# One small store, two issuers: splitting the last output transfer between SyncE and ScalarE

## The chip, the cores and the metric

The kernel runs on one core of one Trainium2 chip. The metric is the device time of one execution in microseconds; the median of 3 runs of the kernel before is 161.53 us (161.51 to 161.56). A profile of one execution gives the times of single instructions: start and duration on TensorE (PE), VectorE (DVE), ScalarE (ACT), GpSimd (POOL) and SyncE (SP). A "q" behind an engine's name (SPq, ACTq) marks what its sequencer does itself: issuing transfers, waiting, loading a register, branching.

## The reference

The kernel computes a log-sum-exp over the last axis of x, 32 × 512 rows of 1024 floats:

```
max_x = np.max(x, axis=-1, keepdims=True)
return (max_x.squeeze(-1) + np.log(np.sum(np.exp(x - max_x), axis=-1))).astype(np.float32)
```

The input is 67 MB, the output 16384 floats (64 KB).

## The kernel before, in words

The 16384 rows are laid out over 128 partitions, 128 rows to a partition: 112 of them (`W`) form the first part of the output, the last 16 (`B`) the second part. The kernel leaves the maximum out at first: it takes exp of x as it is, sums, takes Ln, and raises a flag if any sum is so small or so large that this was not safe. Only if the flag is raised does it recompute everything with the maximum (the block under `nc.If`, lines 304 to 347).

x comes in by 19 loads (`LOADS`), all issued by SyncE at line 141 into a ring of 48 rows per partition. SyncE waits until the part of the ring that a load overwrites has been used. ScalarE takes the exponential of what has landed, in place (line 229). The sums of a row are then made by one of several ways, written out for each load by letters: VectorE sums whole rows (`R`, line 240), GpSimd adds the halves of rows and VectorE sums the rest (`G`, lines 235 and 159), or VectorE adds the halves and sums in one instruction (`T`, line 167). The very last row is split between VectorE (`a`, line 255) and ScalarE, which sums while it exponentiates (`b`, line 224). There is no planner; the order on each engine is the order of the program text.

The end of the program, in which the change lies, runs as follows. When 112 rows per partition are summed, ScalarE takes their Ln (line 202) and SyncE stores them (line 263). For the last 16, ScalarE takes Ln of 15 (line 267) and then of the last one (line 269), whose two part sums are added by the bias; line 272 copies one part sum to where the flag's arithmetic reads it. SyncE waits for line 269 and issues the last store (line 274): 16 floats from each of 128 partitions, 8 KB, counted on a semaphore `stored` that reaches 16 when it has landed.

Beside that the flag is worked out: VectorE at lines 278 and 282, three matmuls at lines 288, 290 and 292 (the last waits for line 272's copy), and a comparison at line 296. ScalarE and VectorE load the flag into a register (line 299) and branch over the recomputation (line 349 is where both go on). Each raises `done`; SyncE waits for both, waits for the early store, clears the kernel's semaphores (line 352), and at last waits for `stored` to reach 16 and subtracts 16 again (line 354). That wait is SyncE's last instruction in the program.

In the whole of this path SyncE alone issues transfers. ScalarE issues some too, but only inside the recomputation.

Of the kernel before, what the change touches and what calls it, by code (L numbers as in the profile page):

```python
# [53 lines left out]
def kernel(  # L54
# [5 lines left out]
    nc = tc.nc  # L60
# [4 lines left out]
    P = nc.NUM_PARTITIONS  # L65
# [9 lines left out]
    NC = n // P  # L75
    H = d // 2
    W = NC - B
# [5 lines left out]
    out_rest = out_flat[P * W : n].rearrange("(p c) -> p c", p=P)  # L83

    def source(e0, size):
        assert e0 >= W * d or e0 + size <= W * d
        return x_rest[:, e0 - W * d : e0 - W * d + size] if e0 >= W * d else x_rows[:, e0 : e0 + size]
# [9 lines left out]
    def sbuf(name, cols, dtype=fp32, rows=P):  # L97
        return nc.alloc_sbuf_tensor(name, [rows, cols], dtype).ap()
# [6 lines left out]
    res = sbuf("res", NC)  # L105
# [10 lines left out]
    act = Counted(nc, nc.scalar, "act")  # L116
# [9 lines left out]
    stored = nc.alloc_semaphore("stored")  # L126
# [53 lines left out]
    for i, (size, parts) in enumerate(loads):  # L180
# [8 lines left out]
        for k, part in enumerate(parts):  # L189
# [8 lines left out]
            if part[0][0] == "L":  # L198
# [4 lines left out]
                    out=res[:, 0:W], in_=sumexp[:, 0:W], func=AF.Ln  # L203
                ))
                continue
            if part[0][0] == "A":
                assert here == p
                for _ in range(part[0][1]):
                    v = ring[:, p : p + d]
                    summed_by_act = act.did(nc.scalar.activation(  # L210
                        out=v, in_=v, func=AF.Exp, accum_out=sumexp[:, c : c + 1]
# [11 lines left out]
            if part[-1][0] == "b":  # L223
                nc.scalar.activation(  # L224
                    out=v, in_=v, func=AF.Exp, accum_out=rest
# [5 lines left out]
            for how, s in part:  # L231
                rows = ring[:, p : p + s * d].rearrange("p (c d) -> p c d", d=d)
                if how == "G":
                    pool.wait(act, at)
                    folded.append((c, p, s, pool.did(nc.gpsimd.tensor_tensor(  # L235
                        out=rows[:, :, 0:H], in0=rows[:, :, 0:H], in1=rows[:, :, H:d], op=ALU.add,
                    ))))
                elif how == "R":
                    dve.wait(act, at)
                    users.append((p, p + s * d, dve, dve.did(nc.vector.reduce_sum(  # L240
                        out=sumexp[:, c : c + s], in_=rows, axis=AX.X
# [27 lines left out]
    ln_last = act.did(nc.scalar.activation(  # L269
        out=res[:, LAST:NC], in_=rest, func=AF.Ln, bias=sumexp[:, LAST:NC]  # L270
    ))
    last = act.did(nc.scalar.copy(out=sumexp[:, REST : REST + 1], in_=rest))  # L272
    sp.wait(act, ln_last)
    nc.sync.dma_start(out=out_rest, in_=res[:, W:NC]).then_inc(stored, 16)

    dve.wait(act, summed_by_act)
    nc.vector.wait_ge(parts_summed, 2)
# [1 line left out]
        out=clamped[:, 0 : LEAST + 1 - checked], in0=sumexp[:, checked : LEAST + 1], scalar=LOW,  # L279
# [3 lines left out]
        out=total, in_=sumexp[:, checked : TOTAL + 1], axis=AX.X  # L283
# [20 lines left out]
    with nc.If(all_fine < 1):  # L304

        nc.scalar.wait_ge(sp.sem, 16)
        nc.scalar.wait_ge(stored, 16)
        rows = 0
        steps = 0
        for c0 in range(0, NC, RING):  # L310
            s = min(RING, NC - c0)
            v = ring[:, 0 : s * d].rearrange("p (c d) -> p c d", d=d)
            neg = clamped[:, c0 : c0 + s]
            if c0:
                nc.scalar.wait_ge(ready, steps)
            edge = max(c0, min(W, c0 + s))
            for c1, c2 in ((c0, edge), (edge, c0 + s)):
                if c1 == c2:
                    continue
                nc.scalar.dma_start(  # L320
                    out=ring[:, (c1 - c0) * d : (c2 - c0) * d],
                    in_=source(c1 * d, (c2 - c1) * d),
                ).then_inc(again, 16)
                rows += 16
            nc.vector.wait_ge(again, rows)
            nc.vector.tensor_reduce(
                out=neg, in_=v, op=ALU.max, axis=AX.X, negate=True
            ).then_inc(ready, 1)
            nc.vector.wait_ge(ready, steps + 1)
            nc.vector.tensor_add(  # L330
                out=v, in0=v, in1=neg[:, :, None].to_broadcast([P, s, d])
            ).then_inc(ready, 1)
            nc.scalar.wait_ge(ready, steps + 2)
            nc.scalar.activation(out=v, in_=v, func=AF.Exp).then_inc(ready, 1)
            nc.vector.wait_ge(ready, steps + 3)
            nc.vector.reduce_sum(
                out=sumexp[:, c0 : c0 + s], in_=v, axis=AX.X
            ).then_inc(ready, 1)
            steps += 4
        nc.scalar.wait_ge(ready, steps)  # L340
        nc.scalar.activation(out=res, in_=sumexp[:, 0:NC], func=AF.Ln).then_inc(ready, 1)
        nc.vector.wait_ge(ready, steps + 1)
        nc.vector.tensor_sub(out=res, in0=res, in1=clamped).then_inc(ready, 1)
        nc.scalar.wait_ge(ready, steps + 2)
        nc.scalar.dma_start(out=out_rest, in_=res[:, W:NC]).then_inc(again, 16)
        nc.scalar.dma_start(out=out_rows, in_=res[:, 0:W]).then_inc(again, 16)
        nc.scalar.wait_ge(again, rows + 32)
# [5 lines left out]
    kind = dict(sync_type="semaphore", id=stored.num, ant_name="stored")  # L353
    nc.sync.add_instruction(mybir.InstEventSemaphore(
        name=nc.get_next_instruction_name(), engine=mybir.EngineType.SP,
        sync_info=mybir.SyncInfo(
            on_wait=[mybir.SyncWait(wait_mode="sem-ge-imm", wait_value=16, **kind)],
            on_update=[mybir.SyncUpdate(update_mode="sem-sub-imm", update_value=16, **kind)],
        ),
    ))  # L360

# [46 lines left out]
```

## Time and profile before

| what | us |
|---|---|
| median of 3 runs | 161.53 |
| the profiled execution | 161.49 |
| its span, first to last instruction of the program | 160.2 |
| VectorE busy | 116.2 |
| ScalarE busy | 114.6 |
| GpSimd busy | 33.3 |
| last store, start of its issue | 158.70 |
| last store, from issue to landing | 1.4 |

The span is what the profile's rows cover; 161.49 less 160.2 leaves 1.3 us that lie around it and that no row shows. The transfers of x fill nearly all of the span: 67.18 MB on one queue, whose packets took 97.9% of the 16 DMA engines' span. In the view of the chain, time is followed back from the instruction that ended last on a computing engine; what SyncE and the sequencers do after that is read from other views: the instructions of one line, the waits of SyncE, and the timeline.

### The profile page before, as it was taken

Reading aid. Unit: us, or ns where it says so; the run is one execution under the profiler, and the core shown is the slowest. Engines: PE = TensorE matmul, PEld = TensorE weight load, DVE = VectorE, ACT = ScalarE, POOL = GpSimd, SP = SyncE. Lnnn points to the kernel's source line nnn. Section 1 sums busy time; section 2 is a strip of 40 time slices with the busy share of each in tenths; the row PEclk is TensorE's granted clock in tenths of the full one; section 3 lists DMA queues with packets and bytes.
Section 4 is the critical chain, followed back from the end, with each engine's and each line's share of the span. In section 5 each row is a group of like instructions: output and inputs, shape, how many; then the busy total and the mean of one; then the engine's idle time right before and its main releaser. Section 6 shows DMA issues by size and latency. Waiting matters only on the chain.

```text
span 160.2 us, 183 instructions
## 1 busy us (share of the span) xinstructions
PE 0.3 (0%) x6; PEld 0.2 (0%) x6; DVE 116.2 (73%) x56; ACT 114.6 (72%) x32; POOL 33.3 (21%) x14
## 2 busy tenths in 40 slices
PE   0000000000000000000000000000000000000000
PEld 0000000000000000000000000000000000000000
DVE  0000000029997599999999699929999999999996
ACT  3000069970999419992799349964998999999996
POOL 0000000000000000000000000990580589996000
DMA  8997999799699699996999999997989999999993
GB/s 272 496 512 336 432 515 466 306 515 498 272 513 513 272 479 478 478 463 268 453 468 468 468 430 430 430 430 332 499 364 472 415 446 395 451 395 431 414 408 105
DMA packets 3025, 67.18 MB, mean 419 GB/s; under 512 B 592, under 2 KB 720, under 8 KB 1488
## 3 DMA queue, kind: packets, MB, share of 16 engines
q1 hardware_dynamic: 3024, 67.18, 97.9%
q14 instruction: 1, 0.01, 0.0%
HBM read 67.11 MB, written 0.07 MB: 419 GB/s over the span
## 4 chain that ended last, share of the span: by engine, by line
DMA 53%; ACT 21%; DVE 18%; POOL 5%; issue 0%; PE 0%; SPq 0%
DMA ring<-in_x_dram 53%; ACT ring L229 21%; DVE sumexp L240 15%; POOL ring L235 5%; DVE sumexp L159 2%; ACT ring L224 0%; SPq L141 0%; DVE clamped L278 0%; PE count L288 0%; ACT res L202 0%; DVE fine L296 0%; PE count L290 0%; PE count L292 0%
## 5 line engine op out<-in xcount | busy, mean ns | idle before, releaser
L229 ACT ACTIVATE ring<-ring 128x16000 f32<-128x16000 f32 (+24 forms) x25 | 112.2, 4546 | 42.7 <-DMA ring<-in_x_dram 42.6
L240 DVE TENSOR_REDUCE sumexp<-ring 128x9 f32<-128x9216 f32 (+7 forms) x10 | 89.8, 9000 | 39.1 <-ACT ring L229 39.1
L235 POOL TENSOR_TENSOR ring<-ring 128x2048 f32<-128x2048 f32 (+5 forms) x8 | 33.0, 4128 | 112.3 <-ACT ring L229 112.2
L159 DVE TENSOR_REDUCE sumexp<-ring 128x4 f32<-128x2048 f32 (+5 forms) x8 | 16.5, 2079 | 3.4 <-POOL ring L235 3.4
L167 DVE SCALAR_TENSOR_TENSOR ring<-ring 128x512 f32<-128x512 f32 (+1 forms) x16 | 9.8, 672 | 0.0
L128 ACT ACT_TABLE_LOAD x1 | 1.3, 1283 | 1.4 <-PEq L63 1.4
L167 DVE DVE_READ_ACCUMULATOR ring<-ring 128x1 f32 x16 | 1.3, 82 | 0.0
L224 ACT ACTIVATE ring<-ring 128x480 f32<-128x480 f32 x1 | 0.6, 602 | 0.0
L288 PE MATMUL count<-far,bad 128*1 128x1 f32 x2 | 0.2, 165 | 158.7 <-DVE clamped L278 158.7
L176 DVE TENSOR_REDUCE sumexp<-sumexp 128x1 f32<-128x106 f32 x2 | 0.4, 260 | 0.0
L296 DVE TENSOR_SCALAR fine<-count 1x1 int32<-1x1 f32 x1 | 0.1, 146 | 0.3 <-PE count L292 0.3
L129 POOL MEMSET ones<- 128x1 f32 x1 | 0.1, 98 | 1.0 <-POOLq L63 1.0
L288 PEld LDWEIGHTS count<-far,bad 128*1 128x1 f32 x2 | 0.1, 82 | 158.7 <-DVE clamped L278 158.7
L202 ACT ACTIVATE res<-sumexp 128x112 f32<-128x112 f32 x1 | 0.3, 280 | 0.0
L269 ACT ACTIVATE res<-rest,sumexp 128x1 f32<-128x1 f32 x1 | 0.3, 261 | 0.0
L278 DVE SCALAR_TENSOR_TENSOR clamped<-sumexp 128x23 f32<-128x23 f32 x1 | 0.2, 183 | 0.1
L267 ACT ACTIVATE res<-sumexp 128x15 f32<-128x15 f32 x1 | 0.2, 205 | 0.0
L290 PE MATMUL count<-total,ones 128*1 128x1 f32 x2 | 0.2, 164 | 0.0
L292 PE MATMUL count<-sumexp,ones 128*1 128x1 f32 x2 | 0.2, 164 | 0.0
L282 DVE TENSOR_REDUCE total<-sumexp 128x1 f32<-128x24 f32 x1 | 0.2, 173 | 0.0
L224 ACT ACTIVATION_READ_ACCUMULATOR ring<-ring 128x1 f32 x1 | 0.2, 153 | 0.0
L272 ACT COPY sumexp<-rest 128x1 f32<-128x1 f32 x1 | 0.2, 151 | 0.0
(8 smaller groups left out, 0.8 us busy)
## 6 DMA issues: line engine op xcount, KB each, us to landing
ring<-in_x_dram SPq DMA_DIRECT2D x1, 8048.0 KB, 38.9
ring<-in_x_dram SPq DMA_DIRECT2D x1, 8016.0 KB, 57.5
ring<-in_x_dram SPq DMA_DIRECT2D x1, 8000.0 KB, 21.4
ring<-in_x_dram SPq DMA_DIRECT2D x1, 7472.0 KB, 25.8
ring<-in_x_dram SPq DMA_DIRECT2D x1, 7312.0 KB, 23.0
ring<-in_x_dram SPq DMA_DIRECT2D x1, 6720.0 KB, 21.6
ring<-in_x_dram SPq DMA_DIRECT2D x1, 5200.0 KB, 17.6
ring<-in_x_dram SPq DMA_DIRECT2D x1, 3584.0 KB, 19.1
```

The lines of the kernel that those rows point to most:

```text
L128: nc.scalar.preload_act_table_set("natural_log_exp_and_others")
L159: at = dve.did(nc.vector.reduce_sum(out=sumexp[:, c0 : c0 + s], in_=half, axis=AX.X))
L167: return nc.vector.scalar_tensor_tensor(out=lo, in0=lo, scalar=1.0, in1=v[:, h : 2 * h], op0=ALU.mult, op1=ALU.add, accum_out=sumexp[:, co ...
L176: dve.did(nc.vector.tensor_reduce(out=sumexp[:, col : col + 1], in_=sumexp[:, 0:c], op=op, axis=AX.X))
L202: ln_early = act.did(nc.scalar.activation(out=res[:, 0:W], in_=sumexp[:, 0:W], func=AF.Ln))
L224: nc.scalar.activation(out=v, in_=v, func=AF.Exp, accum_out=rest).then_inc(parts_summed, 1)
L229: at = act.did(nc.scalar.activation(out=v, in_=v, func=AF.Exp))
L235: folded.append((c, p, s, pool.did(nc.gpsimd.tensor_tensor(out=rows[:, :, 0:H], in0=rows[:, :, 0:H], in1=rows[:, :, H:d], op=ALU.add,))))
L240: users.append((p, p + s * d, dve, dve.did(nc.vector.reduce_sum(out=sumexp[:, c : c + s], in_=rows, axis=AX.X))))
L267: act.did(nc.scalar.activation(out=res[:, W:LAST], in_=sumexp[:, W:LAST], func=AF.Ln))
L269: ln_last = act.did(nc.scalar.activation(out=res[:, LAST:NC], in_=rest, func=AF.Ln, bias=sumexp[:, LAST:NC]))
L288: pe.did(nc.tensor.matmul(count, lhsT=bad, rhs=far, start=True, stop=False))
```

## The change

The last store is cut at partition 64. SyncE issues partitions 0 to 63 as before, after its wait for line 269. ScalarE, after the same wait on its own semaphore, issues partitions 64 to 127 on its own queue; in its program this stands behind the copy of line 272 and ahead of the load of the flag. Both halves count on the semaphore `stored`, which therefore reaches 32; the two waits for it and the subtraction at the end are changed to 32.

```
     last = act.did(nc.scalar.copy(out=sumexp[:, REST : REST + 1], in_=rest))
     sp.wait(act, ln_last)
-    nc.sync.dma_start(out=out_rest, in_=res[:, W:NC]).then_inc(stored, 16)
+    half = P // 2
+    nc.sync.dma_start(out=out_rest[0:half], in_=res[0:half, W:NC]).then_inc(stored, 16)
+    act.wait(act, ln_last)
+    nc.scalar.dma_start(out=out_rest[half:P], in_=res[half:P, W:NC]).then_inc(stored, 16)
...
-        nc.scalar.wait_ge(stored, 16)
+        nc.scalar.wait_ge(stored, 32)
...
-            on_wait=[mybir.SyncWait(wait_mode="sem-ge-imm", wait_value=16, **kind)],
-            on_update=[mybir.SyncUpdate(update_mode="sem-sub-imm", update_value=16, **kind)],
+            on_wait=[mybir.SyncWait(wait_mode="sem-ge-imm", wait_value=32, **kind)],
+            on_update=[mybir.SyncUpdate(update_mode="sem-sub-imm", update_value=32, **kind)],
```

## The prediction

> **What bounds the kernel now.** I read the page's chain first, to see whether the edit lies on it at all.
>
> ```profile
> span 160.2 us, 183 instructions
> q1 hardware_dynamic: 3024, 67.18, 97.9%
> DMA 53%; ACT 21%; DVE 18%; POOL 5%; issue 0%; PE 0%; SPq 0%
> ```
>
> The loads of x bound the run (53% of the chain, one queue whose packets fill 97.9% of 16 engines' span); nothing there changes. The edit touches only what follows the last exponential, so the question is about the last two microseconds. That stage stands in the chain in order of time (start, length, what), here from 157 us on, and in the timeline of 158.2 to 160.2 us:
>
> ```profile
> 157.78 0.61 ACT ring L224 x2
> 158.39 0.02 issue
> 158.41 0.20 DVE clamped L278 x2
> 158.62 0.04 issue
> 158.66 0.19 PE count L288 x2
> 158.85 0.09 PE count L290 x2
> 158.94 0.07 PE count L292 x2
> 159.00 0.02 issue
> 159.03 0.15 DVE fine L296
> ```
>
> ```profile
> 158.28 0.20 ACT L267 ACTIVATE res<-sumexp 128x15 f32<-128x15 f32 x1
> 158.41 0.26 ACT L269 ACTIVATE res<-rest,sumexp 128x1 f32<-128x1 f32 x1
> 158.57 0.15 ACT L272 COPY sumexp<-rest 128x1 f32<-128x1 f32 x1
> 158.70 0.34 SPq L274 DMA_DIRECT2D out_dram<-res  x1
> ```
>
> Two paths leave L269. One is the flag: L278, the matmuls, L296, then steps that the chain leaves out because they belong to the sequencers. The other is the store, issued by SyncE at 158.70 for 0.34 us. Which ends last is told by the instructions of lines 299, 349, 352 and 354 (duration in ns three times, first and last start), by SyncE's waits, and by the DMA view:
>
> ```profile
> L299 ACTq TENSOR_LOAD <-fine x1: 468/468/468, 159.2 to 159.2; - x1
> L349 ACTq EVENT_SEMAPHORE  x1: 17/17/17, 159.9 to 159.9; - x1
> L352 SPq EVENT_SEMAPHORE_RANGE_CLEAR  x1: 87/87/87, 159.9 to 159.9; - x1
> L354 SPq EVENT_SEMAPHORE  x1: 17/17/17, 160.1 to 160.1; - x1
> ...
> SPq L352 <- ACTq L349: 0.8, 1, 0.8
> SPq L354 <- SPq L354: 0.2, 1, 0.2
> ...
> out_dram<-res SPq DMA_DIRECT2D x1, 8.0 KB, 1.4
> ```
>
> The flag path ends when SyncE has cleared its semaphores, at 159.9 + 0.087 = 160.0. Then SyncE still waits 0.2 us (rounded) at L354, the wait for the semaphore `stored`, and what it waits for is the store: 158.70 + 1.4 = 160.1. So the store ends last, but by only 0.1 to 0.2 us; I use 0.13 (160.12 less 159.99). That is the most that any faster store can win here. Work on the flag or on PE is covered.
>
> Where the store's 1.4 us go is seen by cutting the tail into windows (length, busy time of PE, PEld, DVE, ACT and POOL, clock, DMA share, GB/s), and by counting packets from 159.04 on:
>
> ```profile
> 158.70:159.04 0.34, 0.29 (x6) 0.18 (x6) 0.01 (x1) 0.03 (x1) 0.00 (x0) 1.00 0.00 0
> 159.04:159.54 0.50, 0.00 (x0) 0.00 (x0) 0.13 (x1) 0.00 (x0) 0.00 (x0) 1.00 0.00 0
> 159.54:159.76 0.22, 0.00 (x0) 0.00 (x0) 0.00 (x0) 0.00 (x0) 0.00 (x0) 1.00 0.42 38
> 159.76:160.16 0.40, 0.00 (x0) 0.00 (x0) 0.00 (x0) 0.00 (x0) 0.00 (x0) 1.00 0.00 0
> ...
> q1 hardware_dynamic: 144, 0.01, 7.9%
> ```
>
> Issue 0.34, then 0.50 until the first packet, 0.22 in which all 144 packets run, about 0.36 until the last semaphore step is in. Only 0.22 of 1.42 us depends visibly on how much is stored; the engines are 42% busy in it, and idle on both sides.
>
> **The change, part by part.**
>
> SyncE's half. It still waits for L269 and still starts at 158.70. Its issue now names 64 partitions. No row has an issue of 64, but rows have many of 128: after a wait they take about 0.33 us whatever their size, and one that directly follows another takes more.
>
> ```profile
> L141 SPq DMA_DIRECT2D ring<-in_x_dram x12: 327/328/440, 51.2 to 132.9; - x12
> L141 SPq DMA_DIRECT2D ring<-in_x_dram x5: 328/434/469, 132.1 to 133.9; - x5
> L141 SPq DMA_DIRECT2D ring<-in_x_dram x1: 386/386/386, 0.0 to 0.0; - x1
> ```
>
> (First and second rows are the issues from 51 to 133 us and from 132 to 134.4 us; the third is the run's very first.) I keep 0.34. Its data packets are 64 instead of 128: between 0.11 us (half) and 0.22 (both halves interleave on the same engines). So this half lands at 158.70 + 0.34 + 0.50 + (0.11 to 0.22) + 0.36 = 160.01 to 160.12: a gain between 0.11 and nothing.
>
> ScalarE's half. The new wait is on ScalarE's own L269 and stands behind L272. In order, L272 is issued first, so the matmul L292 that reads its copy isn't delayed. The transfer can begin when L269's result is signalled, that is where SyncE's begins, 158.70, and I take the copy's end, 158.72. Behind it on ScalarE's queue is one thing, the load of the flag (L299), which starts at 159.2 once L296 ends at 159.18. The queue is free for 159.2 − 158.72 = 0.48 us, so an issue of up to 0.48 us costs the flag nothing. If it took longer, the flag's load, the branch and SyncE's clear would move by the excess; the first 0.13 us of that disappears in SyncE's wait for the store.
>
> How long ScalarE's issue takes no row shows, for ScalarE issues no transfer in this trace. The near rows are SyncE's: 0.33 (alone), 0.39 (the first of the run), 0.43 to 0.47 (behind another). Farther off, ScalarE's only step of this kind is the flag's load, 0.47. I take 0.39, as this is the first transfer that ScalarE issues and its queue has carried nothing. For the rest I keep the store's own row: 0.50 + 0.22 + 0.36 = 1.08. The half lands at 158.72 + 0.39 + 1.08 = 160.19, against 160.12 before: +0.07 us.
>
> Bounds of that half. Lower: issue 0.33 from 158.70, packets 0.11, landing 160.00, so that SyncE's clear at 159.99 ends the kernel: −0.13. Upper without queueing: issue 0.47, and until the first packet what the run's first load took, since that is the only start of an unused queue shown:
>
> ```profile
> 0.39:1.01 0.62, 0.00 (x0) 0.00 (x0) 0.00 (x0) 0.00 (x0) 0.05 (x2) 1.00 0.00 0
> ```
>
> (no packet from the end of its issue, 0.39, to 1.01). It reads HBM where the store reads SBUF, so 0.62 is an end, not my value. Landing 158.72 + 0.47 + 0.62 + 0.22 + 0.36 = 160.39: +0.27.
>
> The counts of 32. SyncE's last wait counts both halves and its subtraction stays one instruction of 17 ns: nothing. The other wait for 32 is in the recomputation, which this input doesn't enter (ScalarE's line 349 signals at 159.9, right behind its branch): nothing. Semaphore steps double from 16 to 32; they are small packets inside the 0.22, which I left whole for that reason.
>
> Sum: the later half decides, +0.07 on the profiled execution's 161.49, which is 161.56. The median of the runs shown is 161.53, 0.04 above it: 161.60. The 1.3 us of the execution that lie outside the span I take as unchanged; no row shows them.
>
> A rule against the change: the Trainium skill, "DMA: Bandwidth & Descriptors", section "Rules for kernel authors", says of two transfers to disjoint halves of the partitions not to bother, since both spread over all 16 engines and serialize. By it nothing could be won in the 0.22 us; the trace's 42% share there leaves open whether interleaved packets would need all of it.
>
> **The rivals.**
>
> 1. *The second transfer is handled behind the first (slower).* The two issues fall on the same moment. Where SyncE issues back to back, each takes 0.43 to 0.47 rather than 0.33, so something behind the issue takes one transfer at a time for a while. If that is shared by the two queues, ScalarE's issue finishes after SyncE's (159.04) plus 0.44: 159.48; + 1.08 = 160.56, +0.44, giving 161.97. It becomes "slower" once the half lands 0.32 late, that is when ScalarE's issue ends past 159.36. The flag's load would then start 0.28 late and stay hidden under the store. Against it: the slowing is seen on one engine's own queue only, and may be that engine's.
>
> 2. *ScalarE is simply slow to issue (slower).* Its one unusual step with a long row is the table load:
>
> ```profile
> L128 ACT ACT_TABLE_LOAD  x1: 1283/1283/1283, 1.4 to 1.4; - x1
> ```
>
> With an issue of that length the half lands at 158.72 + 1.28 + 1.08 = 161.08, +0.96: 162.49. Against it: on its flag load and semaphore steps ScalarE's sequencer is as quick as the others.
>
> 3. *Half the packets, half the time (no change by the bound, but below before).* With 0.33 to issue and 0.11 for the packets the store drops off the end and the clear bounds: −0.13, 161.40. For it: the engines' 42%. Against it: the same 144 packets and more on the same engines, and only 0.13 to win.
>
> **How the numbers follow.** About 0.2% (0.32 us) is what a measurement of this kernel can tell from no change. My forecast, a later half by 0.07 with its own range 161.40 to 161.85: 0.43. Rival 3 lies inside the same bound: 0.13. Rival 1: 0.29. Rival 2: 0.12. Something outside this reckoning that is faster by over 0.32 us: 0.03, since the flag path caps the gain at 0.13. That makes same 0.56, slower 0.41, faster 0.03. The range runs from rival 3's 161.40 past rival 1's 161.97 to 162.15, and leaves out most of rival 2 and the little below: under 2 in 10.
>
> **What would show it.** A second hardware queue with about 80 packets; a ScalarE DMA issue at about 158.7 (by its place to L269) of 0.33 to 0.47 us and landing 1.4 to 1.5 after it; the flag's load still 0.5 behind the copy; SyncE's last wait a little over 0.2. An issue of ScalarE that ends 0.4 behind SyncE's, or a landing of 1.7 or more, shows rival 1; an issue of a microsecond, and a late flag load, rival 2; no wait left at SyncE's last instruction, rival 3. The prediction is wrong if ScalarE's transfer has a cost that SyncE's rows don't share, or if use of a second queue lengthens what lies outside the span.

## The result, and the profile after

The split kernel takes 162.36 us (median of 6 runs, 162.22 to 162.54) against 161.55 us before on the same chip: ratio 1.0052, 95% interval 1.0042 to 1.0063. It is slower by 0.8 us, outside the forecast's range (161.40 to 162.15), and past the 0.2% that was called "no change".

The page of the split kernel: span, and the two hardware queues (packets, MB, share of 16 engines).

```profile
span 160.9 us, 184 instructions
q1 hardware_dynamic: 2960, 67.17, 97.4%
q10 hardware_dynamic: 80, 0.00, 0.0%
```

The second queue with 80 packets (64 of data, 16 semaphore steps) is there, as intended. The timeline of its tail:

```profile
158.63 0.26 ACT L269 ACTIVATE res<-rest,sumexp 128x1 f32<-128x1 f32 x1
158.92 0.53 SPq L275 DMA_DIRECT2D out_dram<-res  x1
158.93 0.56 ACTq L277 DMA_DIRECT2D out_dram<-res  x1
```

Both issues begin where the one issue began, just after L269. But they take 0.53 and 0.56 us where the whole store took 0.34. In the DMA view the landings are 1.7 and 2.0 us after the issue, against 1.4:

```profile
out_dram<-res SPq DMA_DIRECT2D x1, 4.0 KB, 1.7
out_dram<-res ACTq DMA_DIRECT2D x1, 4.0 KB, 2.0
```

Windows of the tail, cut at the ends of the issues and of the packets (length, busy time of PE, PEld, DVE, ACT, POOL, clock, DMA share, GB/s):

```profile
158.92:159.48 0.56, 0.29 (x6) 0.18 (x6) 0.14 (x1) 0.03 (x1) 0.00 (x0) 1.00 0.00 0
159.48:160.09 0.61, 0.00 (x0) 0.00 (x0) 0.00 (x0) 0.00 (x0) 0.00 (x0) 1.00 0.00 0
160.09:160.28 0.19, 0.00 (x0) 0.00 (x0) 0.00 (x0) 0.00 (x0) 0.00 (x0) 1.00 0.23 22
160.28:160.37 0.09, 0.00 (x0) 0.00 (x0) 0.00 (x0) 0.00 (x0) 0.00 (x0) 1.00 0.00 0
160.37:160.56 0.19, 0.00 (x0) 0.00 (x0) 0.00 (x0) 0.00 (x0) 0.00 (x0) 1.00 0.24 22
160.56:160.93 0.37, 0.00 (x0) 0.00 (x0) 0.00 (x0) 0.00 (x0) 0.00 (x0) 1.00 0.00 0
```

SyncE's packets run from 160.09 to 160.28, then nothing moves for 0.09 us, and ScalarE's run from 160.37 to 160.56. They don't overlap, and each 80 packets take about as long as the 144 did before. From the end of its issue ScalarE's half waits 0.89 us for its first packet (159.48 to 160.37) and SyncE's 0.64 (159.45 to 160.09), where the whole store waited 0.50.

The flag path, by the instructions of lines 302, 352, 355 and 357:

```profile
L302 DVEq TENSOR_LOAD <-fine x1: 536/536/536, 159.4 to 159.4; - x1
L302 ACTq TENSOR_LOAD <-fine x1: 950/950/950, 159.5 to 159.5; - x1
L352 ACTq EVENT_SEMAPHORE  x1: 17/17/17, 160.7 to 160.7; - x1
L355 SPq EVENT_SEMAPHORE_RANGE_CLEAR  x1: 81/81/81, 160.7 to 160.7; - x1
L357 SPq EVENT_SEMAPHORE  x1: 17/17/17, 160.9 to 160.9; - x1
```

ScalarE's load of the flag, 0.47 us before, takes 0.95; VectorE's load of the same word is as it was (0.54, 0.55 before). SyncE's clear thus ends at 160.79, still 0.11 us ahead of the landing of ScalarE's half at 160.90 (the lead was 0.13 before). Counted from the start of SyncE's issue, both paths moved back together: the landing by 0.56 us and the clear by 0.58.

Where the time went, in the two profiled executions (161.49 and 162.50 us, a difference of 1.01): SyncE's issue starts 0.22 later (158.92 against 158.70), which comes from the stream of loads ahead of the edit: the last of them lands at 157.92 against 157.70. That 0.22 is mostly chance: averaged over the runs, the spans of the two kernels differ by 0.64, and the tail makes up 0.56 of that. From that issue to the end of the span are 2.01 us instead of 1.45: 0.56. And the execution is 1.57 us longer than its span instead of 1.34: 0.23. The last two, 0.79, are the loss that the medians show (0.81).

### The profile page after: what moved, and what is told of

Its sections match the earlier page's. It is cut to its first block, busy times and chain, and to the rows that moved or that the text cites. A ratio compares the mean times of both kernels' runs of the same rounds, so it can differ in the third digit from the quotient of the medians.

```text
span 160.9 us, 184 instructions
## 1 busy us (share of the span) xinstructions
PE 0.3 (0%) x6; PEld 0.2 (0%) x6; DVE 116.2 (72%) x56; ACT 114.6 (71%) x32; POOL 33.3 (21%) x14
## 4 chain that ended last, share of the span: by engine, by line
DMA 53%; ACT 21%; DVE 18%; POOL 5%; issue 0%; PE 0%; SPq 0%
DMA ring<-in_x_dram 53%; ACT ring L229 21%; DVE sumexp L240 15%; POOL ring L235 5%; DVE sumexp L159 2%; ACT ring L224 0%; SPq L141 0%; DVE clamped L281 0%; PE count L291 0%; ACT res L202 0%; DVE fine L299 0%; PE count L293 0%; PE count L295 0%
## 5 line engine op out<-in xcount | busy, mean ns | idle before, releaser
L269 ACT ACTIVATE res<-rest,sumexp 128x1 f32<-128x1 f32 x1 | 0.3, 261 | 0.0
```

The source lines that it names most:

```text
L269: ln_last = act.did(nc.scalar.activation(out=res[:, LAST:NC], in_=rest, func=AF.Ln, bias=sumexp[:, LAST:NC]))
```

## The experiments

Each is an edit of the kernel before or of the split kernel. The theories that I started with: A, the two issues collide in something shared; B, ScalarE's queue is slow by itself, or its first use is; C, the 0.23 us outside the span go with the use of a second queue.

**The whole store by ScalarE.**

```
-    sp.wait(act, ln_last)
-    nc.sync.dma_start(out=out_rest, in_=res[:, W:NC]).then_inc(stored, 16)
+    act.wait(act, ln_last)
+    nc.scalar.dma_start(out=out_rest, in_=res[:, W:NC]).then_inc(stored, 16)
```

> The whole last store (128 partitions) goes out from ScalarE alone, in the place where the split kernel issues its half; SyncE issues nothing there. Theory A (the two issues collide: what handles a transfer behind the issue is shared): with no second issue beside it ScalarE's issue falls from 0.56 to about 0.34 us, lands 1.4 to 1.5 us after its start, and the flag's load is back at 0.47 us. Rival B (ScalarE's queue is slow by itself): the issue stays at 0.5 us or more, landing 1.9 to 2.0, the flag's load 0.95. Theory C (use of a second hardware queue lengthens what lies outside the span): the execution less its span is 1.55 us, as in the split kernel, against 1.34 before; if C is wrong it is 1.34. Time by A and C 161.8, by A without C 161.55, by B and C 162.3.

Measured: 161.81 us against 161.48, ratio 1.0021 (1.0011 to 1.0031). Its issue in the timeline and its flag load:

```profile
158.76 0.38 ACTq L274 DMA_DIRECT2D out_dram<-res  x1
```

```profile
L299 ACTq TENSOR_LOAD <-fine x1: 472/472/472, 159.3 to 159.3; - x1
```

An issue of 128 partitions by ScalarE takes 0.38, 0.03 to 0.04 more than SyncE's, and the flag's load is 0.47. So ScalarE isn't slow by itself, and B falls in that form. The tail is only 0.03 longer than before, yet the run loses 0.33: over its 10 runs the time exceeds the span by 1.60 us on average, against 1.34 over 19 runs of the kernel before. C stands so far.

**Both halves by SyncE.**

```
-    act.wait(act, ln_last)
-    nc.scalar.dma_start(out=out_rest[half:P], in_=res[half:P, W:NC]).then_inc(stored, 16)
+    nc.sync.dma_start(out=out_rest[half:P], in_=res[half:P, W:NC]).then_inc(stored, 16)
```

> Both halves are issued by SyncE, one behind the other, on the one queue. The first issue about 0.33 us, the second about 0.44 by SyncE's rows of back-to-back issues, so the second half lands 0.33 + 0.44 + 0.5 + 0.1 + 0.36 = 1.75 us after the first issue's start, 0.33 later than before. By theory A (one transfer at a time behind the issue) that is about as late as the split kernel's last landing or slightly earlier. The flag's load stays at 0.47 and the part outside the span at 1.34, since ScalarE issues nothing. Time about 161.9; if B alone explained the split kernel, the two halves would cost 0.1 at most, 161.65.

Measured: 162.45 us, ratio 1.0059 (1.0042 to 1.0075); outside the span 1.34.

```profile
158.93 0.53 SPq L275 DMA_DIRECT2D out_dram<-res  x1
159.50 0.59 SPq L276 DMA_DIRECT2D out_dram<-res  x1
```

This missed by half a microsecond. The first issue takes 0.53 although nothing is issued beside it. So neither A nor B explains the long issue: it is there on SyncE alone.

**One transfer by ScalarE early, the last store whole.** In the kernel before:

```
+    early = nc.alloc_semaphore("early")
...
+    spare = sbuf("spare", B)
+    nc.scalar.dma_start(out=spare, in_=x_rest[:, 0:B]).then_inc(early, 16)
     pool.did(nc.gpsimd.memset(ones, 1.0))
...
+    nc.sync.wait_ge(early, 16)
     nc.sync.wait_ge(sp.sem, 16)
```

> The kernel before with its one last store by SyncE, and one small extra load (64 bytes for each partition, into a tile that nobody reads) issued by ScalarE at the start, where ScalarE waits for the first load anyway. The tail is as before: landing 1.4, flag load 0.47. Theory C: outside the span 1.55 us instead of 1.34, time 161.75. Without C: 161.55.

Measured: 161.84 us, ratio 1.0023 (1.0013 to 1.0032). The tail is as before (issue 0.34, landing 1.4). Outside the span lie 1.59 us on average over 10 runs. So the part outside needs no split and no late transfer, only that ScalarE issues one somewhere.

**The split kernel with that early transfer.** The edit is the same, made to the split kernel.

> The split kernel with the same small extra load on ScalarE's queue at the start, so that the last half is no longer the first transfer of its queue. Theory A: no change, ScalarE's issue 0.56, landing 2.0, flag load 0.95, time 162.35. Rival B in the form that the queue's first use is dear: issue near 0.4, landing 1.5, flag load 0.5, time 161.8.

Measured: 162.60 us, ratio 1.0071 (1.0054 to 1.0087). Issues 0.53 and 0.55, flag load 0.94. That ScalarE's transfer was the first of its queue isn't the cause; B is out in both forms. Outside the span lie 1.72 us, now that ScalarE issues two transfers. I hadn't expected that, and it leaves the time 0.25 above the 162.35 expected for A.

**ScalarE's half behind its flag load.**

```
-    act.wait(act, ln_last)
-    nc.scalar.dma_start(out=out_rest[half:P], in_=res[half:P, W:NC]).then_inc(stored, 16)
...
+    act.wait(act, ln_last)
+    nc.scalar.dma_start(out=out_rest[half:P], in_=res[half:P, W:NC]).then_inc(stored, 16)
     nc.vector.sem_inc(done, 1)
```

> The split kernel with ScalarE's half issued only after ScalarE has loaded the flag, that is 0.9 us behind SyncE's half. Theory A: apart from each other both issues take about 0.34 us and land 1.3 to 1.4 after their start, and the flag's load is 0.47; the second half then lands at about the old end of the tail + 0.95, time 162.3 to 162.5 with C. Rival B: ScalarE's issue stays at 0.55 and its landing at 2.0 even alone, time near 163.

Measured: 163.05 us, ratio 1.0092 (1.0075 to 1.0109).

```profile
158.75 0.53 SPq L275 DMA_DIRECT2D out_dram<-res  x1
159.76 0.55 ACTq L305 DMA_DIRECT2D out_dram<-res  x1
```

A whole microsecond apart, both issues are as long as side by side. Each lands after 1.7 us: here ScalarE's 2.0 becomes 1.7. The time is the one expected for B, but not for B's reason: SyncE's issue is long as well, and ScalarE's landing did not stay at 2.0.

**SyncE's half alone.** The kernel before with `out_rest[0 : P // 2]` and `res[0 : P // 2, W:NC]` in its last store; the other half of the last 16 columns is not written.

> Only partitions 0 to 63 of the last store go out, by SyncE; the other half of the last 16 columns is left out of the output. It shows what an issue of 64 partitions and its landing cost alone. Theory A: issue 0.33, landing 1.3 to 1.4 (half the packets), so the 0.53 and 1.7 in the split kernel come from the neighbour. Were 64 partitions dear in themselves, the issue would stay near 0.53 and the first packet 0.64 behind it. Time 161.45 to 161.55, since the flag path ends only 0.13 earlier.

Measured: 161.75 us, ratio 1.0015 (1.0006 to 1.0025): storing half costs more than storing all. Its issue in the timeline and its landing in the DMA view:

```profile
158.70 0.53 SPq L274 DMA_DIRECT2D out_dram<-res  x1
```

```profile
out_dram<-res SPq DMA_DIRECT2D x1, 4.0 KB, 1.7
```

With no second transfer at all, the issue is 0.53 and the landing 1.7 as in the split kernel. So theory A doesn't explain SyncE's half; a transfer of 64 partitions is dear in itself (D).

**ScalarE's half alone.** The kernel before with its last store replaced by `nc.scalar.dma_start(out=out_rest[P // 2 : P], in_=res[P // 2 : P, W:NC])` behind ScalarE's wait; the other half of those columns is not written.

> ScalarE issues its half (partitions 64 to 127) alone; the other half of the last 16 columns is left out of the output. Theory D (a transfer of 64 partitions is dear in itself, wherever it is issued): issue 0.55 us, first packet 0.64 behind its end, landing 1.75, against 0.89 and 2.0 in the split kernel, where it also queues behind SyncE's half. The flag's load, which starts right behind the issue, ends about 0.1 us after the first packet of this queue in all runs so far: by that it takes 0.7 us here, not 0.95. Theory A (collision alone): issue 0.38, landing 1.45, flag load 0.47.

Measured: 162.14 us, ratio 1.0039 (1.0023 to 1.0055). Windows from the issue's start, its end, and the first packet to the last:

```profile
158.82:159.37 0.55, 0.28 (x6) 0.17 (x6) 0.15 (x1) 0.02 (x1) 0.00 (x0) 1.00 0.00 0
159.37:160.01 0.64, 0.00 (x0) 0.00 (x0) 0.00 (x0) 0.00 (x0) 0.00 (x0) 1.00 0.00 0
160.01:160.20 0.19, 0.00 (x0) 0.00 (x0) 0.00 (x0) 0.00 (x0) 0.00 (x0) 1.00 0.24 22
```

```profile
L299 ACTq TENSOR_LOAD <-fine x1: 713/713/713, 159.4 to 159.4; - x1
```

As theory D said: 0.55, 0.64 to the first packet, and a flag load of 0.71. So of the 0.89 us in the split kernel 0.64 belong to the 64 partitions and 0.25 to the neighbour; that much of theory A remains. From the start of the issue to the end of the span are 1.75 us here, against 1.45 before and 2.01 in the split kernel. The flag's load again ends 0.1 after the first packet of ScalarE's queue (160.12 after 160.02), as in the split kernel (160.47 after 160.37).

**Shapes one at a time.** Behind everything else SyncE stores the same results again, each store waited for, so the 175.56 us of its one execution hold nine extra stores. The edit is nine pairs like this one:

```
+    nc.sync.dma_start(out=out_rest[0:64], in_=res[0:64, W:NC]).then_inc(probe, 16)
+    nc.sync.wait_ge(probe, 32)
```

> The kernel before, and behind everything a chain of extra stores by SyncE, one at a time, each waited for, that write the same results again: 128 partitions of 16 columns, 0 to 63, 64 to 127, 32, 96 and 16 partitions of 16 columns, then 64 and 128 partitions of 112 columns, and 128 partitions of 8 columns. Theory D: 128 partitions take 0.33 to 0.34 us to issue and land in 1.4 whatever the columns; 64 take 0.53 and land in 1.7 whatever the columns and whichever half. 32, 96 and 16 tell whether it is the count (then between, or falling with it) or any count other than 128 (then all about 0.53). Theory A: all issues 0.33.

The timeline, in the order of that list:

```profile
160.41 0.33 SPq L354 DMA_DIRECT2D out_dram<-res  x1
161.83 0.53 SPq L356 DMA_DIRECT2D out_dram<-res  x1
163.54 0.47 SPq L358 DMA_DIRECT2D out_dram<-res  x1
165.21 0.35 SPq L360 DMA_DIRECT2D out_dram<-res  x1
166.57 0.33 SPq L362 DMA_DIRECT2D out_dram<-res  x1
167.97 0.32 SPq L364 DMA_DIRECT2D out_dram<-res  x1
169.28 0.47 SPq L366 DMA_DIRECT2D out_dram<-res  x1
171.05 0.35 SPq L368 DMA_DIRECT2D out_dram<-res  x1
172.63 0.35 SPq L370 DMA_DIRECT2D out_dram<-res  x1
```

128 partitions take 0.33 to 0.35 whatever the columns. Those of 64 (lines 356, 358 and 366) take 0.47 to 0.53. But 32, 96 and 16 partitions (lines 360, 362, 364) take 0.32 to 0.35, so D as I had put it, in either of its two readings, is wrong: of the five counts tried it is 64 alone. From the end of the issue to the first packet, here for line 356 (64 partitions) and line 354 (128):

```profile
162.36:163.00 0.64, 0.00 (x0) 0.00 (x0) 0.00 (x0) 0.00 (x0) 0.00 (x0) 1.00 0.00 0
160.74:161.23 0.49, 0.00 (x0) 0.00 (x0) 0.00 (x0) 0.00 (x0) 0.00 (x0) 1.00 0.00 0
```

The trace gives 0.64 to 0.65 for the three of 64 and 0.49 to 0.50 for all others; from the start of the issue to the landing 1.65 to 1.76 against 1.29 to 1.57. Theory E: the count 64 is dear.

**Split by columns.** In the split kernel:

```
-    half = P // 2
-    nc.sync.dma_start(out=out_rest[0:half], in_=res[0:half, W:NC]).then_inc(stored, 16)
+    mid = W + B // 2
+    nc.sync.dma_start(out=out_rest[:, 0 : B // 2], in_=res[:, W:mid]).then_inc(stored, 16)
...
-    nc.scalar.dma_start(out=out_rest[half:P], in_=res[half:P, W:NC]).then_inc(stored, 16)
+    nc.scalar.dma_start(out=out_rest[:, B // 2 : B], in_=res[:, mid:NC]).then_inc(stored, 16)
```

> The last store is split by columns instead of partitions: SyncE stores 8 columns of all 128 partitions, ScalarE the other 8. Theory D: both issues 0.34 to 0.38, the later landing 1.45 to 1.6, flag load near 0.47; with the 0.23 outside the span that goes with a transfer of ScalarE, 161.8 to 161.9. Theory A: issues 0.53 to 0.56, landing 2.0, 162.35.

Measured: 161.92 us, ratio 1.0027 (1.0016 to 1.0037), just past the upper end of the expectation. Issues 0.34 and 0.38, flag load 0.48.

```profile
159.33:159.79 0.46, 0.00 (x0) 0.00 (x0) 0.09 (x1) 0.00 (x0) 0.00 (x0) 1.00 0.00 0
159.79:159.98 0.19, 0.00 (x0) 0.00 (x0) 0.00 (x0) 0.00 (x0) 0.00 (x0) 1.00 0.76 40
159.98:160.04 0.06, 0.00 (x0) 0.00 (x0) 0.00 (x0) 0.00 (x0) 0.00 (x0) 1.00 0.23 11
160.04:160.56 0.52, 0.00 (x0) 0.00 (x0) 0.00 (x0) 0.00 (x0) 0.00 (x0) 1.00 0.00 0
```

Here the packets of both queues overlap: 288 of them run in 0.25 us, with the engines 76% busy for most of it. Only the last stretch, from the last packet to the end, is longer than before: 0.52 against 0.40.

**Cut at partition 96.** In the split kernel `half = 96`.

> The split kernel with the cut at partition 96 instead of 64: SyncE stores 96 partitions, ScalarE 32. Theory E (it is the count 64 that is dear: 0.47 to 0.53 us to issue and 0.65 to the first packet, against 0.32 to 0.35 and 0.49 for 16, 32, 96 and 128): issues 0.33 and 0.38, landings 1.4 to 1.55, the flag's load 0.47 to 0.5, the span 0.5 below the split kernel's; with the 0.23 outside the span, 161.75 to 161.9. Against E (two issuers at once are dear): issues over 0.5, landing near 2.0, 162.35.

Measured: 161.87 us against 161.51, ratio 1.0021 (1.0011 to 1.0030). Timeline and DMA view:

```profile
158.96 0.36 SPq L275 DMA_DIRECT2D out_dram<-res  x1
158.97 0.40 ACTq L277 DMA_DIRECT2D out_dram<-res  x1
```

```profile
out_dram<-res SPq DMA_DIRECT2D x1, 6.0 KB, 1.4
out_dram<-res ACTq DMA_DIRECT2D x1, 2.0 KB, 1.6
```

The same change with another place for the cut: issue to end of span 1.60 us (158.96 to 160.56) against 2.01, the flag's load 0.48. E is confirmed in the place where it matters. What is left of the split is 0.15 in the tail and the 0.23 outside. ScalarE's first packet comes 0.50 us after its issue here, and 0.51 in the split by columns, so a neighbour alone does not hold it up. The 0.15 lies behind the last packet: in these two runs, where the packets of both queues overlap, ScalarE's transfer lands 0.48 to 0.49 us after its last packet, against 0.37 for the whole store before and 0.35 in the split kernel (0.57 in the cut at 96 with three early loads, below). Why is not known.

**How many transfers ScalarE issues.** Four, three and five early loads in the kernel before, and three in the split kernel and in the one cut at 96 (four transfers by ScalarE in both). The edit is the early load above, in a loop.

> The kernel before with four small extra loads by ScalarE at its start instead of one. Outside the span lay 1.34 us without a transfer by ScalarE, 1.56 to 1.57 with one, 1.71 with two. If each transfer of that queue counts, 1.95 to 2.0 here and a time of 162.15 to 162.2; if the queue costs once and the 1.71 was chance, 1.57 and 161.8.

> The split kernel (cut at 64) with three small extra loads by ScalarE at the start, so that ScalarE issues four transfers in all. Outside the span lay 1.57 us with one transfer of ScalarE's, 1.71 with two, but 1.34 with four, as with none. If that goes by the number of transfers, 1.34 here, with the tail as in the split kernel (landing 2.0, flag load 0.95). If the last transfer's place in the tail sets it, 1.57 or more.

> The kernel before with three small extra loads by ScalarE at its start (one and four were tried). Outside the span: 1.34 us if three or more of that queue's transfers cost nothing; 1.57 to 1.9 if only a multiple of four costs nothing.

> The same with five. 1.34 us outside the span if four or more cost nothing; 1.57, as with one, if it goes by the remainder after four.

> The cut at partition 96 together with three extra loads by ScalarE at the start, four transfers of ScalarE in all: both dear things of the split are taken away. Landing 1.5 to 1.57, 1.34 us outside the span: 0.1 to 0.15 above before in the tail, and up to 0.3 that the extra loads at the start cost by themselves (the four of the earlier run); 161.6 to 161.9. It should not beat the kernel before.

The time less the span, averaged over all runs of each (a single run's span is on record to 0.1 us):

| transfers by ScalarE | us outside the span | kernels |
|---|---|---|
| none | 1.33 to 1.35 | before; both halves by SyncE; SyncE's half alone |
| 1 | 1.57 to 1.60 | the split kernel; all kernels with one |
| 2 | 1.72 | split with one early load |
| 3 | 1.52 | three early loads, whole store |
| 4 | 1.32 to 1.34 | four early loads; split with three; cut at 96 with three |
| 5 | 1.43 | five early loads, whole store |

For one and for four transfers, which several kernels have, it goes by the number and not by place, size or time of the transfers: three different kernels with four have no extra at all. Two, three and five stand on one kernel each. The expectations were missed here: for four, three and five early loads each named values by some rule, and 1.34, 1.52 and 1.43 were none of them. It isn't simply a remainder after four either (1.43 with five, 1.57 to 1.60 with one), and I have no rule that fits. Times: 161.79 (four early; ratio 1.0018), 162.22 (split with three; 1.0043), 161.96 (three; 1.0031), 161.96 (five; 1.0029) and 161.95 us (cut at 96 with three; 1.0028), the last just above its expectation. The split with three early loads keeps its slow tail (issues 0.53 and 0.55, flag load 0.94). The early loads aren't free in the span: three to five of them make it 0.3 to 0.4 longer in the kernel before and 0.3 in the one cut at 96 (0.1 in the split kernel), and none of these kernels comes near the kernel before.

## Why the prediction was wrong

- *What bounds the tail* was read rightly: the store ends last, with a lead of 0.13 us over the flag path, so that no split could win more. SyncE's half alone shows that this cut could not win even that: half the data didn't land earlier but later, 1.7 against 1.4.
- *"I keep 0.34" for an issue of 64 partitions* is the step that failed. The rows of 128 partitions showed no dependence on size, and I carried that over to another count of partitions. Measured 0.53 on SyncE; and on ScalarE, where I took 0.39 and bounded it by 0.47, 0.56. The 0.47 was no bound even for 128 partitions: of SyncE's 19 issues of x, the rows that I read leave out one of 0.52 us and two of 3.66 and 4.68.
- *"0.50 until the first packet"* is the term that was off the most. It is 0.64 for a half that goes alone, by the same cause, and 0.89 for ScalarE's beside the other half, past the 0.62 that I had as its end. The packets took 0.18 to 0.19 (I had 0.22) and the last part 0.35 (0.36), about as taken. ScalarE's half thus came to 0.56 + 0.89 + 0.18 + 0.35 us.
- *The free 0.48 us on ScalarE's queue*: the order was right, an issue of 0.56 doesn't fit, and the flag's load not only starts 0.1 late but doubles. That the excess stays hidden behind the store is right, with 0.11 to spare.
- *"The 1.3 us … outside the span I take as unchanged"* failed too: +0.23. The prediction named a second queue's cost there as what could make it wrong, without a price.
- *Rival 1* (the second transfer handled behind the first, +0.44) has the size nearest to the tail's 0.56, but its mechanism explains only 0.25 of it. The two issues ran side by side and ended 0.03 apart; the cut at 96 and the cut by columns, with the same two issuers, have no such wait. A landing of 1.7 or more, put down as its sign, doesn't single it out: SyncE's half lands after 1.7 without any neighbour.
- *Rival 2*: ScalarE's issue of a whole store is 0.38, so it is not a slow issuer. *Rival 3* is refuted by SyncE's half alone. Its sign appeared all the same: SyncE's last instruction no longer stands in the list of its waits. That wait got only a little shorter, with the clear 0.11 ahead of the landing where it was 0.13, so the sign told nothing.
- *The skill's rule.* The Trainium skill, "DMA: Bandwidth & Descriptors", section "Rules for kernel authors", advises against two transfers to disjoint halves of the partitions: they serialize, since both use the same 16 engines. The advice holds here: in the split kernel the packets did run one queue after the other, with the engines 23% to 24% busy. Split by columns, though, they overlapped, with 76% of the engines' time in use, so sharing the 16 engines is not by itself what kept the halves apart.

The loss, then, by differences between runs: cutting at 64 and not at 96 costs 0.41 us (2.01 less 1.60 from issue to end of span), two issuers in place of one 0.15 (1.60 less 1.45), and ScalarE's one transfer 0.23 outside the span; together 0.79, where the medians differ by 0.8. These parts are not independent. Taken the other way, ScalarE's half alone lengthens the tail by 0.30 (1.75 less 1.45) and SyncE's half beside it by another 0.26 (2.01 less 1.75); the 0.41 holds the 0.25 that the two halves of 64 cost each other. Each tail is that of one profiled execution.

Not settled: why 64 is dear where 16, 32, 96 and 128 aren't (other counts weren't tried), why two transfers of 64 at once hold each other up, what happens outside the span, which no row shows, and why the flag's load is long behind ScalarE's own transfer of 64. That it waits for that transfer's first packet is not shown: behind 128 or 32 partitions it ends 0.07 to 0.10 us after the first packet, too, but with its usual 0.47 to 0.48 us, and no run changes the load alone.

## What to carry to other kernels

A transfer's fixed cost isn't carried over from rows with another number of partitions: measure the shape that the edit makes. A small store whose time is nearly all fixed (here 1.2 of 1.4 us) has little to gain from being halved. And before an engine is given its first transfer, look at the execution's own time less its span, since a cost can sit where the profile has no rows.

## What the runs showed of the hardware that was not expected

- A store of 64 partitions takes 0.47 to 0.53 us to issue on SyncE (0.55 to 0.56 on ScalarE; 0.59 on SyncE right behind another) and, without a neighbour, 0.64 to 0.65 more to its first packet; with 16, 32, 96 or 128 partitions it is 0.32 to 0.36 on SyncE and 0.49 to 0.50. The bytes of a row play no part in it (64 and 448 tried with 64 partitions; 32, 64 and 448 with 128).
- When SyncE and ScalarE each issue a store of 64 partitions at the same moment, ScalarE's first packet comes 0.88 to 0.89 us after its issue. With 128 partitions each, or 96 and 32, it comes after 0.50 to 0.51.
- Transfers by ScalarE change the time outside the span by their number: +0.23 to 0.26 with one, +0.38 with two, +0.19 with three, nothing with four, +0.1 with five.
- A register load on ScalarE right behind its own transfer of 64 partitions takes 0.71 to 0.95 us instead of 0.47, and ends 0.1 us after that transfer's first packet.
